# Combinations of the last two head pairs moved into the output projection, raw output weights through three fixed buffers

## The chip, the cores and the metric

The kernel runs on 1 core of one Trainium2 chip. The metric is device time in microseconds (us) of one execution of the whole program; of several runs the median is given. A profiled execution is one more run, with its own time. The engines are called as the profile calls them: PE is TensorE (PEld its weight loads), DVE is VectorE, ACT is ScalarE, POOL is GpSimd, SP is SyncE, which issues nearly all DMAs here, in order.

## The reference

One decoder layer for 2048 tokens of width 1024 in float32: a mixer of two groups of heads side by side, then a feed-forward part, then a last norm. Cut to what matters:

```python
def dilated_mixer(q, k, v, rel_bias):            # 8 heads of width 64
    outs, lses = [], []
    for window, dilation in ((128, 1), (512, 4), (2048, 16)):
        o, lse = dilated_branch(q, k, v, rel_bias, window, dilation)
        outs.append(o)
        lses.append(lse)
    w = softmax(stack(lses), axis=0)             # weights of the three branches
    return sum(w[..., None] * stack(outs), axis=0)

def reference(x, ...):
    gq, gk, gv, gr, glow, dq, dk, dv = split(rmsnorm(x) @ w_in)
    o_a = gated_linear_attention(gq, gk, gv, glow)   # "GLA": 4 heads, normed and gated
    o_b = dilated_mixer(dq, dk, dv, rel_bias)
    h = x + concat([o_a, o_b]) @ w_out               # the output projection
    h = h + square(relu(rmsnorm(h) @ w_ff1)) @ w_ff2
    return rmsnorm(h)
```

The step that is moved is the weighted sum at the end of `dilated_mixer`; the weights whose loading changes are `w_out`.

## The kernel before, in words

The kernel has four parts: the input projection, attention, the output projection (with the norm behind it), and the feed-forward part with the last norm. The first and the last issue their instructions in an order written out by hand (`manual_schedule`). In attention and in the output projection, where the change lies, the scheduling framework orders each engine's instructions when the program is built: the order of the code gives priorities, a model of times says what is ready, and `tc.keep_in_program_order` (lines 1042, 1048, 1055) pins an instruction to its place on its engine. On the chip each engine then runs its own list strictly in order.

**Precision.** Large matrix products are made of three: each operand is split into a high part (ACT, a copy to fp32r) and a low part (DVE, the rest), and `mm3` (lines 131 to 134) adds high x high, low x high and high x low in a PSUM bank. PSUM banks have tags; tag "o", used by GLA, has one bank.

**Memory.** Most SBUF tiles come from one pool of 26 equal slots (`slot`, line 119). An instruction whose tile has no free slot waits until an earlier tile's last reader is done.

**Attention** runs 160 units of four or two blocks of 128 queries. In round k, unit k + 3 gets its scores (lines 964, 966; DVE adds the bias and finds the extreme in L976, ACT takes the exponential in L977), unit k is transposed (L986, evicted in L993 or L995) and unit k - 2 is multiplied with the values (L1005, evicted in L1008 to a tile O per pair of heads and branch). Heads go in pairs `pr` 0 to 3, with branches `br` 2, 1, 0. `plan` holds other work by round (`at_unit`). Steps of GLA, one chain of small products, are mixed in at a fixed rate: L1131 starts a step's decay in the bank of tag "o", L1191 (DVE) reads the previous product from it.

**Combination.** When a pair of heads has its three branches, `combine` (line 1033) sums them with their weights, for n tiles of 128 tokens from tile t0. Branches 1 and 2 come back from DRAM (`combine_load`, L1030, tile `cmb`); branch 0 is still in O. The steps are: the minimum M of the three stored extremes (DVE, L1042, L1043), differences (L1045), Exp (ACT, L1048), the sum of weighted denominators Z (L1049 to L1052), its reciprocal (DVE, L1055), the weights (L1057), then for each four tiles three products (L1063) and two sums (L1065) of 128x512 elements, and for pairs 0 to 2, or the upper half of pair 3, a store to `mixD` in DRAM. All but M, Exp and the reciprocal run on POOL, except for tiles 12 to 15 of pair 3, which run on DVE (`W`, `X`). `combine` is a generator: each call of `step` (line 1257) runs it to the next `yield`. Pairs 0 to 2 are combined while the next pair is in attention (line 1283, eight tiles at a time), pair 3 in four pieces of four tiles at the end (line 1291).

**Output weights.** `load_wo` (line 1199) is called eight times, every third unit from unit 132 on. Each call takes a slot for the raw block, loads it (L1203) and splits it (ACT L1205 or L1208, DVE L1206 or L1209).

**Output projection.** Tiles go in the order 0, 4, 1, 5, 2, 6, 3, 7, then 8, 12, and so on; `mix_T` loads a tile one step ahead (L1393, L1394, tile `mx`), transposes it (L1385; for tokens below 1024 the last 128 columns come straight from pair 3's O) and splits it into `mT` (ACT L549, DVE L550). The product is lines 132 to 134 with the tiles `wo` and `mT`, the sum with x is L1554. After each tile `norm_to_T` normalizes the tile before it: square on ACT (L168), a power of -1/2 on POOL (L163), scaling on DVE (L170), transposes (L1385), copies `bb` (L1348). The feed-forward part follows; it isn't touched.

Of the kernel before, what the change touches and what calls it, by code (L numbers as in the profile page):

```python
# [18 lines left out]
D = 1024  # L19
# [87 lines left out]
def emit(tc, a, stop=99):  # L107
# [924 lines left out]

    def combine(pr, t0, n, loaded, X):

        ts = slice(t0, t0 + n)
        R = [outs[pr, 0][:, ts], *[r[:, t0 % 8:t0 % 8 + n] for r in loaded]]
        at = small[:, t0 // 4 % 2 * 48:] if n == 4 else small
        E, Z, M = view(at, (3, n, 2)), view(at[:, 6 * n:], (2, n, 2)), view(at[:, 10 * n:], (n, 2))
        nm = [r[:, :, 130:132] for r in R]
        den = [r[:, :, 0:130:129] for r in R]  # L1040
        W = V if (pr, t0) == (3, 12) else G
        tc.keep_in_program_order(V.tensor_tensor(M, nm[0], nm[1], op=OP.min))  # L1042
        V.tensor_tensor(M, M, nm[2], op=OP.min)  # L1043
        for b in range(3):
            W.tensor_tensor(E[:, b], M, nm[b], op=OP.subtract)  # L1045
        if pr < 3:
            yield
        tc.keep_in_program_order(A.activation(E, E, AF.Exp))  # L1048
        W.tensor_tensor(Z[:, 0], E[:, 0], den[0], op=OP.mult)  # L1049
        for b in (1, 2):  # L1050
            W.tensor_tensor(Z[:, 1], E[:, b], den[b], op=OP.mult)
            W.tensor_tensor(Z[:, 0], Z[:, 0], Z[:, 1], op=OP.add)  # L1052
        if pr < 3:
            yield
        tc.keep_in_program_order(V.reciprocal(Z[:, 1], Z[:, 0]))  # L1055
        for b in range(3):
            W.tensor_tensor(E[:, b], E[:, b], Z[:, 1], op=OP.mult)  # L1057
        yield
        for t in range(0, n, 4):
            rs = [r[:, t:t + 4, 1:129].rearrange("p t (h e) -> p t h e", h=2) for r in R]  # L1060
            for b, r in enumerate(rs):
                wb = E[:, b, t:t + 4].unsqueeze(3).to_broadcast([128, 4, 2, 64])
                X.tensor_tensor(r, r, wb, op=OP.mult)  # L1063
                if b:
                    X.tensor_tensor(rs[0], rs[0], r, op=OP.add)  # L1065
                    yield
        if pr < 3 or t0 >= 8:
            issue_later(3 if pr < 3 else 2,
                        mixD[:, 512 + 128 * pr:640 + 128 * pr].rearrange("(t p) n -> p t n", p=128)[:, ts],
                        R[0][:, :, 1:129])  # L1070
# [127 lines left out]

    def load_wo(n):
        for c in range(len(WO), len(WO) + n):  # L1200
            raw = slot("woraw")[:, :D]
            w = view(slot("wo", FR), (2, D))
            SP.dma_start(raw, wo[:, c])  # L1203
            if c < 4:
                A.activation(w[:, 0], raw, AF.Copy, scale=gn[:, c:c + 1])  # L1205
                V.scalar_tensor_tensor(w[:, 1], raw, gn[:, c:c + 1], w[:, 0].bitcast(F32), op0=OP.mult, op1=OP.subtract)  # L1206
            else:
                A.activation(w[:, 0], raw, AF.Copy)  # L1208
                V.tensor_tensor(w[:, 1], raw, w[:, 0].bitcast(F32), op=OP.subtract)  # L1209
            WO.append(w)  # L1210

# [37 lines left out]

    got, running = {}, {}  # L1250

    def combine_at(pr, t0, n, at, steps):

        if at is not None:
            at_unit(at + AHEAD, lambda: got.update({(pr, t0 // 8): combine_load(pr, t0 // 8)}))

        def step():
            if (pr, t0) not in running:
                running[pr, t0] = combine(pr, t0, n, got[pr, t0 // 8], V if (pr, t0) == (3, 12) else G)
            next(running[pr, t0], None)  # L1260

        for k in steps:
            at_unit(k + AHEAD, step)

    for pr in range(4):
# [3 lines left out]
        for hh, br in seq:  # L1269
# [7 lines left out]
            if br == 2 and first:  # L1277
                pieces = load_head(b.h)
                for n in (13, 11, 8):
                    at_unit(first - n, lambda p: next(p), pieces)  # L1280
                if hh == 0:
                    for half in range(2):
                        combine_at(pr - 1, 8 * half, 8, first - 2 + 7 * half, [first + 4 + 7 * half + n for n in range(8)])
            if (pr, br) != (3, 0):
                for n in range(0, NT, m):
                    units.append(Unit(b, range(n, n + m)))
            elif hh:
                for n in range(0, NT, 4):
                    for w in (was, b):
                        units.extend(Unit(w, range(n + k, n + k + 2)) for k in (0, 2))  # L1290
                for n, at in ((0, 8), (4, 11), (8, 14), (12, 18)):
                    combine_at(3, n, 4, first + 5 + n // 8 if n % 8 == 0 else None, [first + at + k for k in range(4)])
            was = b
    NU = len(units)
    for i in range(8):
        at_unit(NU - 28 + 3 * i + AHEAD, load_wo, 1)
    gla = gla_steps()
# [240 lines left out]
    nxt = mix_T(tiles[0])  # L1538
    late = None
    back = []  # L1540
    for at, t in enumerate(tiles):
# [13 lines left out]
        SP.dma_start(hD[t * 128:t * 128 + 128], h)  # L1555
        if late is not None:
            norm_to_T(*late)
        if back:
# [5 lines left out]
        if at == W1AT + 1:  # L1564
# [6 lines left out]
            sum1(0, 1)  # L1571
        late = (h, u[:, 0], t)

# [177 lines left out]
    with tc.manual_schedule(engines={SP.engine}):  # L1751
# [3 lines left out]
        for at in range(7):  # L1755
            if at == 2:
                norm_to_T(*late)
            if back:
# [120 lines left out]
```

## Time and profile before

| what | value |
|---|---|
| median of 3 runs | 2266.61 us (2266.53 to 2270.08) |
| profiled execution | 2268.76 us |
| its span, first to last instruction | 2267.0 us |
| busy time of ACT, DVE, POOL | 1163.6, 1628.3, 800.3 us |
| mean granted PE clock | 0.995 of full speed |
| attention's last value products (L1005) | end at about 858.5 us |
| output projection | from 858.4 to about 1070 us |

Rows of a timeline give the start in us from the span's start, the busy time in us, the engine, the line of the kernel, the operation, the tile written and the tiles read, shapes and count; in square brackets stands how long the engine was idle before it and what ended that. In the list of waits, a row gives who waited, for whom, the total in us, how often, and the longest. In a table of stretches, each engine's busy time stands with the number of its instructions, then the granted PE clock (1.00 is full speed), the mean busy share of the DMA engines, and GB/s. Groups give the count, the total busy time and the mean of one in ns, then idle time before them.

### The profile page before, as it was taken

What the parts mean: (1) busy time and instruction counts of PE and PEld (TensorE: products, weight loads), DVE (VectorE), ACT (ScalarE), POOL (GpSimd) and SP (SyncE); (2) the same over time, 40 slices, a digit from 0 to 9 for tenths busy, and PEclk for the clock granted to TensorE, in tenths of its full rate; (3) what the DMA queues carried; (4) which work ended last, traced back from release to release, by engine and by line L of the source; (5) the groups of instructions that cost most, each with busy time, mean ns of one, the idle gap of its engine ahead of it and who ended that gap; (6) DMA issues with size and microseconds to landing.
All of it is one profiled execution on the core that took longest, in us unless ns stands there. A gap on an engine that the chain in (4) does not pass through costs nothing.

```text
span 2267.0 us, 34335 instructions
## 1 busy us (share of the span) xinstructions
PE 2235.2 (99%) x12324; PEld 1928.8 (85%) x12324; DVE 1628.3 (72%) x2773; ACT 1163.6 (51%) x2088; POOL 800.3 (35%) x786
## 2 busy tenths in 40 slices
PE   9999999999999998999999999999999999999998
PEld 7978998899999997888888887888888788888886
DVE  6866767746677685446677779777776878758897
ACT  5554446425777772224655557555562333323544
POOL 2111000115478775000032335232345536332665
PEclk9999999999999999999999999999999999999999
DMA  7256444757757864777444456544488554454563
GB/s 206 87 176 194 131 136 153 251 175 236 229 186 252 270 196 144 222 229 260 131 151 140 149 195 206 154 138 150 137 271 313 192 166 135 148 160 156 169 222 112
DMA packets 308268, 415.24 MB, mean 183 GB/s; under 512 B 19509, under 2 KB 236126, under 8 KB 302464
## 3 DMA queue, kind: packets, MB, share of 16 engines
q1 hardware_dynamic: 307950, 412.77, 56.9%
q8 instruction: 97, 1.59, 0.3%
q14 instruction: 75, 0.61, 0.1%
q10 hardware_dynamic: 146, 0.27, 0.0%
HBM read 268.48 MB, written 149.20 MB: 184 GB/s over the span
## 4 chain that ended last, share of the span: by engine, by line
PE 88%; DVE 5%; DMA 2%; issue 2%; ACT 1%; POOL 1%; SPq 0%; POOLq 0%; ACTq 0%; DVEq 0%
PE ps_a L133 10%; PE ps_a L134 10%; PE ps_a L132 10%; PE ps_c L132 8%; PE ps_c L134 8%; PE ps_c L133 8%; PE ps_a L1005 5%; PE ps_d L134 4%; PE ps_d L132 4%; PE ps_d L133 4%; PE ps_d L986 3%; PE ps_c L966 2%; PE ps_c L964 2%; PE ps_o L132 2%; DVE ct L1650 2%
## 5 line engine op out<-in xcount | busy, mean ns | idle before, releaser
L1429 ACT ACTIVATE w1comb<-w1raw 128x512 fp32r<-128x512 f32 x224 | 141.4, 632 | 243.7 <-PE ps_a L134 81.8
L1608 ACT ACTIVATE cs<-rs 128x1024 fp32r<-128x1024 f32 x104 | 109.6, 1055 | 222.9 <-PE ps_c L134 127.9
L1434 DVE TENSOR_TENSOR w1comb<-w1raw,w1comb 128x512 fp32r<-128x512 f32 x224 | 175.8, 786 | 27.3 <-ACT w1comb L1429 27.3
L977 ACT ACTIVATE pe<-pe,O 128x256 f32<-128x256 f32 (+1 forms) x384 | 156.2, 454 | 58.0 <-DVE O L976 53.3
L1005 PE MATMUL ps_a<-v,pt 128*128 128x65 f32 x1200 | 180.3, 252 | 0.0
L1005 PEld LDWEIGHTS ps_a<-v,pt 128*128 128x128 f32 x1200 | 174.9, 194 | 1.1
L986 PE MATMUL ps_d<-ident,pe 128*128 128x128 f32 x600 | 159.9, 279 | 0.0
L976 DVE CUSTOM_DVE_ANT_0 pe<-ps_c,nb 128x256 f32<-128x256 f32 (+1 forms) x384 | 126.7, 361 | 41.9 <-PE ps_d L986 19.0
L163 POOL TENSOR_TENSOR stats<-stats,mhalf 128x1 f32<-128x1 f32 (+1 forms) x64 | 50.0, 783 | 299.9 <-DVE stats L162 299.9
L132 PE MATMUL ps_a<-hb,w1comb 128*128 128x512 f32 x384 | 149.6, 390 | 0.0
L133 PE MATMUL ps_a<-hb,w1comb 128*128 128x512 f32 x384 | 149.6, 390 | 0.0
L134 PE MATMUL ps_a<-hb,w1comb 128*128 128x512 f32 x384 | 149.4, 389 | 0.0
L1650 DVE TENSOR_TENSOR ct<-rt,ct 128x1024 fp32r<-128x1024 f32 x68 | 137.3, 2019 | 15.7 <-ACT ct L1646 15.4
L134 PE MATMUL ps_c<-ct,cs 128*128 128x512 f32 x360 | 140.1, 389 | 0.0
L132 PE MATMUL ps_c<-ct,cs 128*128 128x512 f32 x360 | 140.1, 389 | 0.0
L133 PE MATMUL ps_c<-ct,cs 128*128 128x512 f32 x360 | 140.1, 389 | 0.0
L918 POOL CAST qp<-qs 128x512 fp32r<-128x512 f32 x64 | 67.2, 1133 | 179.6 <-DVE acc L373 162.6
L1534 POOL TENSOR_TENSOR acc<-acc 128x256 f32<-128x256 f32 x75 | 69.0, 931 | 161.2 <-DVE acc L1534 148.6
L293 ACT ACTIVATE wcomb<-wraw 128x512 fp32r<-128x512 f32 (+2 forms) x119 | 89.2, 755 | 62.0 <-DVE wraw L305 27.0
L1615 DVE SCALAR_TENSOR_TENSOR cs<-rs,cs 128x1024 fp32r<-128x1024 f32 (+1 forms) x56 | 94.1, 1687 | 27.8 <-ACT cs L1608 27.6
L986 PEld LDWEIGHTS ps_d<-ident,pe 128*128 128x128 f32 x600 | 109.5, 187 | 0.3
L1534 POOL TENSOR_TENSOR xt<-acc,acc 128x256 f32<-128x256 f32 x32 | 28.2, 882 | 227.0 <-ACT acc L1496 210.2
(439 smaller groups left out, 7337.7 us busy)
## 6 DMA issues: line engine op xcount, KB each, us to landing
rs<-actD SPq DMA_DIRECT2D x103, 512.0 KB, 3.7
actD<-acc SPq DMA_DIRECT2D x288, 128.0 KB, 2.8
w1raw<-w_ff SPq DMA_DIRECT2D x32, 1024.0 KB, 6.6
rt<-w_ff SPq DMA_DIRECT2D x24, 1024.0 KB, 7.1
k<-kD SPq DMA_DIRECT2D x16, 1024.0 KB, 8.4
rb<-hTD SPq DMA_DIRECT2D x13, 1024.0 KB, 7.8
wraw<-w_in SPq DMA_DIRECT2D x12, 1024.0 KB, 5.4
cmb<-boD SPq DMA_DIRECT2D x16, 528.0 KB, 6.5
```

Source lines behind the costliest of these rows:

```text
L132: T.matmul(out, sh, mh, start=first, stop=False, skip_group_check=more)
L133: T.matmul(out, sl, mh, start=False, stop=False, skip_group_check=more)
L134: T.matmul(out, sh, ml, start=False, stop=last, skip_group_check=more)
L976: V.tensor_tensor_reduce(p, s, bias, scale=1.0, scalar=BIG, op0=OP.add, op1=OP.min, accum_out=nm)
L977: A.activation(p, p, AF.Exp, bias=nm, scale=-1.0)
L986: T.transpose(pb[:, i * 128:i * 128 + 128], src, ident)
L1005: T.matmul(self.b.opsum[:, n % 4], self.pt[:, i * 128:i * 128 + 128], self.b.v[:, blk, cols], start=first, stop=last)
L1429: A.activation(c[:, 0], v, AF.Copy)
L1434: V.tensor_tensor(c[:, 1], v, c[:, 0].bitcast(F32), op=OP.subtract)
L1534: (G if pool or all_pool[0] else V).tensor_tensor(t[l], t[x], t[y], op=OP.add if op == "+" else OP.subtract)
L1608: A.activation(v[:, 0], x, AF.Copy, scale=float(PRODUCTS[ph // 2][2]))
L1650: V.tensor_tensor(v[:, 1], x, v[:, 0].bitcast(F32), op=OP.subtract)
```

## The change

It does five things.

1. The combination of tiles 12 to 15 of pair 3 runs on POOL like all others.
2. The combinations of tokens 1024 to 2047 of pairs 2 and 3 are called from the loop of the output projection: pair 2 (eight tiles) after output tiles 1 to 3, three steps each; pair 3's tiles 8 to 11 after the fourth, and 12 to 15 after the fifth, all four steps at once. Their stores are issued there by a call of `issue` per output tile. The load of pair 2's upper half moves from unit 125 to 148.
3. In pairs 0 to 2 there is one more step, empty, between the sum Z and the reciprocal, and the second half of a pair starts eight units after the first, not seven.
4. The raw output weights no longer take a slot each. They go through three buffers in turn: the tile `xt` (idle in this part) and the halves of one slot.
5. The load of a raw block stands five units ahead of its split.

```diff
-    def combine(pr, t0, n, loaded, X):
+    def combine(pr, t0, n, loaded):
...
-        W = V if (pr, t0) == (3, 12) else G
...
-            W.tensor_tensor(E[:, b], M, nm[b], op=OP.subtract)
+            G.tensor_tensor(E[:, b], M, nm[b], op=OP.subtract)
...
         if pr < 3:
             yield
+        if pr < 3:
+            yield
         tc.keep_in_program_order(V.reciprocal(Z[:, 1], Z[:, 0]))
...
-                X.tensor_tensor(r, r, wb, op=OP.mult)
+                G.tensor_tensor(r, r, wb, op=OP.mult)
                 if b:
-                    X.tensor_tensor(rs[0], rs[0], r, op=OP.add)
+                    G.tensor_tensor(rs[0], rs[0], r, op=OP.add)
                     yield
...
-    def load_wo(n):
-        for c in range(len(WO), len(WO) + n):
-            raw = slot("woraw")[:, :D]
-            w = view(slot("wo", FR), (2, D))
-            SP.dma_start(raw, wo[:, c])
...
+    wo_raws = []
+
+    def load_wo(c):
+        if not wo_raws:
+            t = slot("woraw")
+            wo_raws.extend((xt, t[:, :D], t[:, D:2 * D]))
+        SP.dma_start(wo_raws[c % 3], wo[:, c])
+
+    def split_wo(c):
+        raw, w = wo_raws[c % 3], view(slot("wo", FR), (2, D))
...
         for k in steps:
-            at_unit(k + AHEAD, step)
+            if k < 0:
+                late.setdefault(-k, []).append(step)
+            else:
+                at_unit(k + AHEAD, step)
...
-                        combine_at(pr - 1, 8 * half, 8, first - 2 + 7 * half, [first + 4 + 7 * half + n for n in range(8)])
+                        at = [first + 4 + 8 * half + n for n in range(9)]
+                        combine_at(pr - 1, 8 * half, 8, first - 2 + (8 if pr < 3 else 30) * half,
+                                   at if pr < 3 or not half else [-1, -1, -1, -2, -2, -2, -3, -3, -3])
...
-                for n, at in ((0, 8), (4, 11), (8, 14), (12, 18)):
-                    combine_at(3, n, 4, first + 5 + n // 8 if n % 8 == 0 else None, [first + at + k for k in range(4)])
+                for n, at in ((0, 8), (4, 11), (8, -4), (12, -5)):
+                    combine_at(3, n, 4, first + 5 + n // 8 if n % 8 == 0 else None,
+                               [first + at + k if at > 0 else at for k in range(4)])
...
-        at_unit(NU - 28 + 3 * i + AHEAD, load_wo, 1)
+        at_unit(NU - 33 + 3 * i + AHEAD, load_wo, i)
+        at_unit(NU - 28 + 3 * i + AHEAD, split_wo, i)
...
         SP.dma_start(hD[t * 128:t * 128 + 128], h)
-        if late is not None:
-            norm_to_T(*late)
+        for f in late.get(at + 1, ()):
+            f()
+        issue(clock[0] + 99)
+        if last is not None:
+            norm_to_T(*last)
```

More of the change, by code (lines that the diff above doesn't have):

```diff
@@ L1048, in combine @@
         tc.keep_in_program_order(A.activation(E, E, AF.Exp))
-        W.tensor_tensor(Z[:, 0], E[:, 0], den[0], op=OP.mult)
+        G.tensor_tensor(Z[:, 0], E[:, 0], den[0], op=OP.mult)
         for b in (1, 2):
-            W.tensor_tensor(Z[:, 1], E[:, b], den[b], op=OP.mult)
-            W.tensor_tensor(Z[:, 0], Z[:, 0], Z[:, 1], op=OP.add)
+            G.tensor_tensor(Z[:, 1], E[:, b], den[b], op=OP.mult)
+            G.tensor_tensor(Z[:, 0], Z[:, 0], Z[:, 1], op=OP.add)
+        if pr < 3:
+            yield
         if pr < 3:
@@ L1056, in combine @@
         for b in range(3):
-            W.tensor_tensor(E[:, b], E[:, b], Z[:, 1], op=OP.mult)
+            G.tensor_tensor(E[:, b], E[:, b], Z[:, 1], op=OP.mult)
         yield
@@ L1197, in emit @@
     WO = []
-    def load_wo(n):
-        for c in range(len(WO), len(WO) + n):
-            raw = slot("woraw")[:, :D]
-            w = view(slot("wo", FR), (2, D))
[L1203 to L1210, printed above, removed]
+    wo_raws = []
[6 more added lines that the diff above has]
+        raw, w = wo_raws[c % 3], view(slot("wo", FR), (2, D))
+        if c < 4:
+            A.activation(w[:, 0], raw, AF.Copy, scale=gn[:, c:c + 1])
+            V.scalar_tensor_tensor(w[:, 1], raw, gn[:, c:c + 1], w[:, 0].bitcast(F32), op0=OP.mult, op1=OP.subtract)
+        else:
+            A.activation(w[:, 0], raw, AF.Copy)
+            V.tensor_tensor(w[:, 1], raw, w[:, 0].bitcast(F32), op=OP.subtract)
+        WO.append(w)
     pairs, outs = {}, {}
@@ L1248, in at_unit @@
         plan.setdefault(n, []).append(f)
-    got, running = {}, {}
+    got, running, late = {}, {}, {}
     def combine_at(pr, t0, n, at, steps):
@@ L1258, in step @@
             if (pr, t0) not in running:
-                running[pr, t0] = combine(pr, t0, n, got[pr, t0 // 8], V if (pr, t0) == (3, 12) else G)
+                running[pr, t0] = combine(pr, t0, n, got[pr, t0 // 8])
             next(running[pr, t0], None)
         for k in steps:
-            at_unit(k + AHEAD, step)
+            if k < 0:
+                late.setdefault(-k, []).append(step)
+            else:
+                at_unit(k + AHEAD, step)
     for pr in range(4):
@@ L1538, in emit @@
     nxt = mix_T(tiles[0])
-    late = None
+    last = None
     back = []
@@ L1571, in emit @@
             sum1(0, 1)
-        late = (h, u[:, 0], t)
+        last = (h, u[:, 0], t)
     w2 = a["w_ff2"].rearrange("o (c q p) n -> q p (o c) n", q=4, p=128)
@@ L1756, in emit @@
             if at == 2:
-                norm_to_T(*late)
+                norm_to_T(*last)
             if back:
```

## The prediction

> **What bounds the kernel now.** I read the page first, then who TensorE waited for, then stretches of the span, then the instructions around each of TensorE's two stops.
>
> ```profile
> span 2267.0 us, 34335 instructions
> ...
> PE 2235.2 (99%) x12324; PEld 1928.8 (85%) x12324; DVE 1628.3 (72%) x2773; ACT 1163.6 (51%) x2088; POOL 800.3 (35%) x786
> ```
>
> TensorE (PE) is busy 2235.2 of 2267.0 us. The change leaves its matmuls alone, so it can only win where PE stands still, or where its clock is low after it stood still. In the list of PE's waits, two of the first three lines lie where this change works (the second, L1479, belongs to the feed-forward part):
>
> ```profile
> PE ps_a L133 <- DVE mT L550: 5.6, 1, 5.6
> PE ps_d L132 <- ACT acc L1479: 3.4, 1, 3.4
> PE ps_o L1131 <- issue: 2.7, 1, 2.7
> ```
>
> The stretches (columns: length, busy PE, PEld, DVE, ACT, POOL, granted clock, DMA share, GB/s):
>
> ```profile
> 340.00:820.00 480.00, 480.00 (x3776) 454.91 (x3776) 329.42 (x1096) 298.21 (x739) 220.90 (x307) 1.00 0.67 216
> 831.65:834.30 2.65, 0.00 (x0) 0.03 (x1) 2.38 (x4) 1.53 (x5) 2.65 (x3) 1.00 1.10 351
> 834.30:838.60 4.30, 4.30 (x27) 4.30 (x28) 3.05 (x14) 4.15 (x11) 4.30 (x6) 0.60 1.17 316
> 872.78:877.00 4.22, 4.21 (x12) 3.38 (x13) 0.66 (x2) 0.00 (x0) 3.48 (x6) 0.61 0.44 119
> 905.00:1070.00 165.00, 165.00 (x831) 139.31 (x830) 84.66 (x123) 52.29 (x91) 7.14 (x13) 1.00 0.73 234
> ```
>
> From 340 to 820 (attention) and from 905 to 1070 (output projection) PE never stops and its clock is full: nothing can be won there, and anything new that holds PE up is a loss. The stop at 831.65 costs 2.65 us and then a slow clock, 4.30 us at 0.60: 4.30 x 0.40 = 1.72. After the second stop the clock is 0.61 for 4.21 busy us: 4.21 x 0.39 = 1.64.
>
> **The first stop** is made by the raw output weights; SP's queue, then ACT, DVE and PE:
>
> ```profile
> 825.20 0.57 SPq L1203 DMA_DIRECT2D woraw<-w_out  x1
> ```
>
> ```profile
> 830.78 1.06 ACT L1208 ACTIVATE wo<-woraw 128x1024 fp32r<-128x1024 f32 x1 [2.96 <-DMA woraw<-w_out]
> ```
>
> ```profile
> 831.87 1.56 DVE L1209 TENSOR_TENSOR wo<-woraw,wo 128x1024 fp32r<-128x1024 f32 x1 [2.18 <-ACT wo L1208]
> 833.36 0.84 DVE L1191 TENSOR_TENSOR gla<-gla,ps_o 64x256 f32<-64x256 f32 x2
> ```
>
> ```profile
> 834.30 0.68 PE L1131 MATMUL ps_o<-gla 128*128 128x130 f32 x4 [2.65 <-issue]
> ```
>
> The load goes out at 825.20 and lands 5.6 us later, at a DMA share above 1. ACT waits for it 2.96 us, DVE (in order behind ACT's result) another 2.18, L1191 stands behind DVE's split, and L1131 needs the one ps_o bank that L1191 reads. The trace says only "issue" for that last step; that it is the bank follows from the code and from L1191 ending at 834.20.
>
> **The second stop** is the handoff to the projection. PE, then ACT, DVE and POOL:
>
> ```profile
> 864.72 0.60 PE L1385 MATMUL ps_c<-ident,mx 128*128 128x128 f32 x4
> 865.41 0.33 PE L1385 MATMUL ps_d<-ident,O 128*128 128x128 f32 x1
> 866.49 0.73 PE L132 MATMUL ps_a<-wo,mT 128*128 128x512 f32 x2 [0.75 <-ACT mT L549]
> 872.78 0.80 PE L133 MATMUL ps_a<-wo,mT 128*128 128x512 f32 x1 [5.56 <-DVE mT L550]
> ```
>
> ```profile
> 865.85 0.59 ACT L549 ACTIVATE mT<-ps_d 128x512 fp32r<-128x512 f32 x1
> ```
>
> ```profile
> 870.61 0.68 DVE L550 TENSOR_TENSOR mT<-ps_c,mT 128x512 fp32r<-128x512 f32 x1
> 871.21 0.92 DVE L1065 TENSOR_TENSOR O<-O,cmb 128x512 f32<-128x512 f32 x1
> 872.05 0.68 DVE L550 TENSOR_TENSOR mT<-ps_d,mT 128x512 fp32r<-128x512 f32 x1
> ```
>
> ```profile
> 864.05 1.30 POOL L1065 TENSOR_TENSOR O<-O,cmb 128x512 f32<-128x512 f32 x1
> ```
>
> PE waits for the low part (L550) of tile 0's second half. Its high part was ready at 866.44, so DVE could have begun then; it began at 872.05, because DVE was working off the combination of tokens 1536 to 2047, of which the row at 871.21 is a part, and the low part of another tile (870.61). PE lost 0.75 + 5.56 = 6.31 us. Before that, the transpose of O (865.41) waited for POOL's last add of the combination of tokens 0 to 511, which ended at 864.05 + 1.30 = 865.35.
>
> All that is to be had is 2.65 + 1.72 + 6.31 + 1.64 = 12.3 us.
>
> **Part by part.**
>
> *Weights.* Each load moves five units ahead of its split. From the first of these issues to the one at 835.99 it is six loads, three units apart:
>
> ```profile
> 785.74 0.33 SPq L1203 DMA_DIRECT2D woraw<-w_out  x1
> ```
>
> ```profile
> 829.57 1.61 SPq L1030 DMA_DIRECT2D cmb<-boD  x2
> 831.23 2.60 SPq L1123 DMA_DIRECT2D gla<-gvD  x1
> 833.93 1.96 SPq L1030 DMA_DIRECT2D cmb<-boD  x2
> 835.99 8.95 SPq L1203 DMA_DIRECT2D woraw<-w_out  x2
> 845.43 0.33 SPq L1336 DMA_DIRECT2D gs<-mlp_norm_g  x1
> ```
>
> ```profile
> SPq L1203 <- PE ps_c L966: 10.3, 2, 6.4
> ```
>
> (835.99 - 785.74) / 18 = 2.8 us a unit, so five units are 14 us, against 2.96 us of lateness. The load of block c overwrites the buffer of block c - 3, whose split is planned four units earlier, 11 us. The loads no longer wait on SP for a slot (10.3 us in two waits, with later loads queued behind). So the first stop goes: 4.37 us. If the load is late all the same, nothing of that is won.
>
> *Combination of tokens 1536 to 2047 off DVE, and three combinations behind the first output tiles.* What remains at the handoff is the chain behind POOL: transpose of O 0.33 (from 865.41), ACT 0.59, DVE 0.68, with the small gaps between them at 867.2. PE would run out at 864.72 + 0.60 = 865.3. Left over: 1.9 us instead of 6.31. It is less if POOL ends the combination of tokens 0 to 511 sooner, since the 8-tile combination that fills POOL from 830 to 845 and the one of tokens 1024 to 1535 have gone; at best it is 0. The clock after such a stop costs between 0 and the 1.72 of the 2.65 us stop; I take half, 0.85. So the second stop shrinks from 7.95 to about 2.75 (bounds 0 and 3.6).
>
> The Trainium skill, "TensorE: Matmul & The Clock Gate", section "Why this matters for your kernels", asks for no idle gaps above about 3 us, and its section "What's actually happening" has the clock fall after an idle window of about 3.4 us. This trace disagrees: a stop of 2.65 us was followed by 4.30 us at 0.60. By the page the first stop would be worth 2.65 alone, the leftover stop would cost no clock, and the sum below would be 8.7.
>
> *What those combinations cost later.* On POOL between 780 and 885:
>
> ```profile
> L1065 POOL TENSOR_TENSOR O<-O,cmb 128x512 f32<-128x512 f32 x14 | 19.4, 1392 | 0.1
> L1063 POOL TENSOR_TENSOR cmb<-cmb,small 128x512 f32<-128x512 f32 x14 | 16.2, 1185 | 0.0
> L1063 POOL TENSOR_TENSOR O<-O,small 128x512 f32<-128x512 f32 x7 | 7.2, 1045 | 0.0
> ```
>
> Four tiles cost 1.05 + 2 x 1.19 + 2 x 1.39 = 6.2 us; the three combinations 12.4 + 6.2 + 6.2 = 24.8 us, into a stretch where POOL was busy 7.14 of 165. Who stands behind them is each tile's power of -1/2 (L163), on the way to its normalized transposes:
>
> ```profile
> 893.48 0.56 POOL L163 TENSOR_TENSOR stats<-stats,mhalf 128x1 f32<-128x1 f32 x1 [10.79 <-DVE stats L162]
> ```
>
> ```profile
> 894.07 1.28 DVE L170 SCALAR_TENSOR_TENSOR mx<-mx,stats,gs 128x1024 f32<-128x1024 f32 x1 [0.67 <-POOL stats L163]
> ```
>
> ```profile
> 903.61 0.60 PE L1385 MATMUL ps_c<-ident,mx 128*128 128x128 f32 x4
> ```
>
> The scaled tile is ready at 895.35, the transposes run at 903.61: 8.3 us of cover. Batches of 6.2 fit. The 12.4 us batch, begun at about 892 and taken in one piece ahead of the power, ends at 904.4; power and scale bring it to 906.2: 2.6 us late, once, and up to 1.7 us of clock. I take nothing, since PE may have the next tile's matmuls in hand; 4.3 stays in the range. SP gets three stores more among the projection's loads; the rows they read are first wanted by the ninth tile. The minima, reciprocals and Exps among the output tiles are tiny, and DVE has half of that stretch free.
>
> *The extra step and the shifted combinations of the first pairs* lie where PE never waited (340 to 820): nothing, and with that cover gone at most a stop like the first.
>
> Sum: 4.37 + (7.95 - 2.75) = 9.6 us. The profiled execution took 2268.76 us (its span and 1.76 outside), 2.15 above the median of the runs, 2266.61. It would go to 2259.2, the median to 2257.0.
>
> **The rivals.**
>
> *One stop stays.* The two loads of the 8-tile combination now stand on SP just ahead of those for tokens 0 to 1023, on DMA engines that are full there. If they push them back by one such pair (833.93 - 829.57 = 4.4 us) and POOL's chain with them, PE resumes 4.4 us later than above and the handoff costs 1.9 + 4.4 + 1.64 = 7.9, as before: a gain of 4.4, 2262.2. If the weights are late and the handoff is cured, the gain is 5.2, 2261.4. For it: the DMA share of 1.1 to 1.17. Against: POOL gets 12.4 us of room ahead of that chain. It decides once tokens 0 to 511 are combined later than the 865.35 of now.
>
> *Slots run out: slower.* The pool has 26. When the last scores are issued I count: six for two heads' q and k, v, bias, two rings, four of GLA, branch 0 of the last pair (15); branch 0 of the third pair, three loaded combinations, the raw-weight slot (20); six split weight blocks (26). Full, as now, where SP waits for the scores to end (6.4 us) and goes on at 845.43. The scores free seven, and two weight blocks, the gains and two tiles' mx and mT want seven; but now two of the old holders keep theirs until the third output tile. If another tile's load takes one first and tile 0's transposed halves get theirs only from GLA's four, they come when GLA's last store has landed:
>
> ```profile
> 858.35 0.48 PE L132 MATMUL ps_a<-wo,mT 128*128 128x512 f32 x1
> ```
>
> ```profile
> 873.84 1.54 SPq L1082 DMA_DIRECT2D mixD<-gla  x1
> ```
>
> With the 5.6 us that the load of 825.20 took to land as an estimate for this store, 873.84 + 1.54 + 5.6 + 0.59 + 0.68 = 882.3 in place of 858.35: 23.9 us late, 1.6 of clock, less the 12.3 of both stops: 13.2 slower, 2279.8. It decides from one slot too few at that place; v and the rings, freed as the last values end at about 858.5, speak against it.
>
> *No effect on the order.* The scheduler may run combinations planned among the output tiles earlier, as it runs others later than planned. But minimum, Exp and reciprocal are pinned on DVE and ACT, so POOL can't start before them. I give this no chance of its own.
>
> **How the numbers follow.** Forecast (both stops go or shrink, 2254 to 2261): 0.60. One stop stays (2261 to 2264): 0.22. Slots, slower by over 0.2%: 0.10. Other small stops that eat the gain (2264 to 2270): 0.08. About 0.2%, 4.5 us, is what a measurement of this kernel can tell from no change; 2262.1 is the border. Faster: 0.60, and half of 0.22, less a little for the 4.3 us of the power: 0.69. Slower 0.11, same 0.20. The range goes from 2266.6 - 12.3, less half a us of scatter, to where one stop stays and a small one comes: 2253.8 to 2265.0.
>
> **What would show it.** In the changed profile, right: PE's wait at L1131 gone and L1208's wait for woraw with it; no combination on DVE but minima and reciprocals; the wait for L550 at the handoff 2 us or less; L1063 and L1065 on POOL among the first five output tiles; PE full in the projection. Wrong: a PE stop of over 4 us at the first output matmuls, SP or ACT waiting there for a slot, or PE waiting for transposes of mx with L163 late.

## The result, and the profile after

The changed kernel takes 2256.15 us (median of six runs, 2254.47 to 2256.67) beside 2266.57 us for the kernel before (six runs, 2265.08 to 2270.08): 10.4 us less, ratio 0.9951, 95% interval 0.9941 to 0.9962. The forecast was 2257.0 in a range of 2253.8 to 2265.0. The profiled execution took 2256.31 us, with a span of 2254.5 us.

The head of the page, for the changed kernel:

```profile
span 2254.5 us, 34335 instructions
...
PE 2229.1 (99%) x12324; PEld 1925.5 (85%) x12324; DVE 1605.4 (71%) x2757; ACT 1164.0 (52%) x2088; POOL 812.5 (36%) x802
```

PE runs the same 12324 matmuls and is the bound as before. Sixteen instructions went from DVE to POOL; DVE lost 22.9 us of busy time and POOL gained 12.2.

The list of PE's waits, after (lines are those of the changed kernel: L1398 is the transpose of `mx` or `O` that was L1385, L1189 the GLA product that was L1188, L1492 belongs to the feed-forward part):

```profile
PE ps_d L132 <- ACT acc L1492: 3.4, 1, 3.4
...
PE ps_c L1398 <- DMA mx<-mixD: 2.0, 1, 2.0
```

Both waits at which the forecast aimed are gone: there is no wait for L550 at the handoff, and none at the GLA product L1132 (L1131 before) behind the weights. One is new, 2.0 us for the load of tile 0's `mx`. The table of stretches, after:

```profile
831.00:835.00 4.00, 4.00 (x42) 4.00 (x40) 1.74 (x8) 1.84 (x5) 1.80 (x4) 1.00 1.05 317
...
838.00:853.00 15.00, 12.80 (x116) 12.22 (x115) 11.88 (x38) 10.03 (x23) 11.66 (x29) 1.00 1.08 370
853.00:880.00 27.00, 27.00 (x148) 23.16 (x148) 8.28 (x15) 6.00 (x17) 13.84 (x20) 1.00 0.18 63
880.00:905.00 25.00, 25.00 (x124) 20.87 (x124) 9.63 (x16) 5.45 (x10) 13.68 (x15) 1.00 0.62 193
905.00:1060.00 155.00, 155.00 (x787) 131.14 (x786) 81.90 (x122) 51.46 (x91) 24.54 (x44) 1.00 0.73 236
```

Where PE stood at 831.65 it now runs through. From 853 to 1060, handoff and projection, it never stops, and the clock is full. All that is left is 15.00 - 12.80 = 2.20 us between 838 and 853: 0.2 at L1189 and 2.0 at the transposes of tile 0.

To compare kernels I use two sums. The *stretch* runs from a store at the beginning of attention (L383, at 449.41 in the kernel before) to the last store of `hD`; PE's work in it is the same in every kernel here. The *stops* are what PE loses after that store: I cut 630 us into pieces of 2 us, and for each take 2 less the busy time (idle), and the busy time times 1 less the clock (slow clock). In the profile of before the stops are 9.06 idle + 3.31 slow = 12.37 us, the 12.3 of the prediction; after they are 2.20 + 0 = 2.20. The stretch went from 621.21 to 610.95 us. So 10.2 us of stops answer for 10.3 us of stretch. The two profiled executions differ by 12.45 us; the other 2.2 lie outside: 0.2 ahead of attention, 2.0 in the feed-forward part, which the change does not touch.

### The profile page after: what moved, and what is told of

The parts are those of the page before. It is cut to its first block, busy times and chain, and to the rows that moved or that the text cites. A ratio compares the mean times of both kernels' runs of the same rounds, so it can differ in the third digit from the quotient of the medians.

```text
span 2254.5 us, 34335 instructions
## 1 busy us (share of the span) xinstructions
PE 2229.1 (99%) x12324; PEld 1925.5 (85%) x12324; DVE 1605.4 (71%) x2757; ACT 1164.0 (52%) x2088; POOL 812.5 (36%) x802
## 3 DMA queue, kind: packets, MB, share of 16 engines
q8 instruction: 97, 1.59, 0.3%
## 4 chain that ended last, share of the span: by engine, by line
PE 91%; DVE 4%; issue 2%; DMA 1%; ACT 1%; POOL 0%; SPq 0%; POOLq 0%; ACTq 0%; DVEq 0%
PE ps_a L132 11%; PE ps_a L133 11%; PE ps_a L134 11%; PE ps_c L132 9%; PE ps_c L134 8%; PE ps_c L133 8%; PE ps_a L1005 5%; PE ps_d L133 4%; PE ps_d L132 4%; PE ps_d L134 4%; PE ps_d L986 3%; PE ps_c L966 2%; PE ps_c L964 2%; PE ps_o L132 2%; PE ps_o L134 2%; PE ps_o L133 2%
## 5 line engine op out<-in xcount | busy, mean ns | idle before, releaser
L1666 DVE TENSOR_TENSOR ct<-rt,ct 128x1024 fp32r<-128x1024 f32 x68 | 129.8, 1909 | 18.8 <-ACT ct L1662 18.8
L163 POOL TENSOR_TENSOR stats<-stats,mhalf 128x1 f32<-128x1 f32 (+1 forms) x64 | 50.0, 783 | 242.6 <-DVE stats L162 242.5
L1631 DVE SCALAR_TENSOR_TENSOR cs<-rs,cs 128x1024 fp32r<-128x1024 f32 (+1 forms) x56 | 100.0, 1793 | 29.6 <-ACT cs L1624 29.3
```

The costliest lines, as they stand in the source:

```text
L1631: V.scalar_tensor_tensor(v[:, 1], x, -1.0, v[:, 0].bitcast(F32), op0=OP.mult, op1=OP.subtract)
L1666: V.tensor_tensor(v[:, 1], x, v[:, 0].bitcast(F32), op=OP.subtract)
```

## The experiments

My theory: PE's two stops are the whole cost; the weights' part removes the first, GpSimd's part the second, and the gains add up. The rivals: one of the stops stays or comes back in another place, GpSimd is the new bound, or the combinations in the projection cost something. Each kernel's ratio is to runs of the kernel before on the same chip; the groups of runs were made on different chips, so ratios are compared and not medians. Stretch and stops are those of one execution, the profiled one. The row "before" is the profile that the prediction read.

| kernel | ratio to before, 95% interval | idle | slow clock | stops | stretch |
|---|---|---|---|---|---|
| before | 1 | 9.06 | 3.31 | 12.37 | 621.21 |
| w_only | 0.9995 [0.9987, 1.0004] | 7.37 | 3.57 | 10.94 | 621.42 |
| g_only | 0.9969 [0.9961, 0.9978] | 6.38 | 1.57 | 7.95 | 617.06 |
| w_and_g | 0.9981 [0.9973, 0.9990] | 5.81 | 1.60 | 7.41 | 618.50 |
| c_only | 0.9960 [0.9948, 0.9972] | 3.78 | 2.58 | 6.36 | 613.74 |
| p3_moved | 0.9976 [0.9968, 0.9985] | 3.94 | 1.70 | 5.64 | 616.13 |
| p2_moved | 0.9968 [0.9955, 0.9980] | 3.31 | 1.59 | 4.90 | 613.78 |
| no_step | 0.9960 [0.9948, 0.9972] | 3.20 | 1.58 | 4.78 | 613.22 |
| late_load | 0.9967 [0.9955, 0.9979] | 3.19 | 1.47 | 4.66 | 613.53 |
| after_again | 0.9953 [0.9940, 0.9965] | 3.02 | 1.58 | 4.60 | 613.42 |
| loads_later | 0.9957 [0.9943, 0.9970] | 1.79 | 1.69 | 3.48 | 612.11 |
| gains_later | 0.9951 [0.9938, 0.9964] | 2.64 | 0.00 | 2.64 | 611.47 |
| one_batch | 0.9957 [0.9945, 0.9969] | 2.58 | 0.00 | 2.58 | 611.23 |
| the change | 0.9951 [0.9941, 0.9962] | 2.20 | 0.00 | 2.20 | 610.95 |

An interval is some 5 us wide, so the ratios part the first kernels from the last; to tell 2 us apart takes the stops and the stretch. These come from single executions: the changed kernel itself had 2.20 us of stops in one and 4.60 in another. The profiled executions of c_only and p3_moved were the slowest of theirs (3.8 and 4.3 us above the median), though some 3 us of that lie outside the stretch and in none of these sums; that of late_load was its fastest (2.1 below).

### The weights alone (w_only)

The kernel before, with parts 4 and 5 of the change (three fixed buffers, load five units ahead of split) and nothing else:

```diff
-            raw = slot("woraw")[:, :D]
+            t = slot("woraw")
+            wo_raws.extend((xt, t[:, :D], t[:, D:2 * D]))
...
-        at_unit(NU - 28 + 3 * i + AHEAD, load_wo, 1)
+        at_unit(NU - 33 + 3 * i + AHEAD, load_wo, i)
+        at_unit(NU - 28 + 3 * i + AHEAD, split_wo, i)
```

> The kernel before with the change to the weights alone: three fixed buffers, and each load five units ahead of its split; all combinations where they were. My theory (the first stop is the late landing of a raw block, the second is DVE's combination ahead of L550): the stop at L1131 is gone, the handoff still waits some 5.6 us for L550: 2266.6 - 4.4 = 2262.2 us. Rival (the first stop comes from GpSimd's and the DMA engines' load of the 8-tile combination at that time, and the wait for the weights only hides it): the stop stays in another form, 2265.5 to 2267.

Measured: no change, 0.9995, where I had expected 4.4 us. The first stop is gone, but nearly nothing is won. PE's waits in this kernel (L1391 is the transpose of tile 0's last columns from `O`):

```profile
PE ps_a L133 <- DVE mT L550: 2.7, 1, 2.7
PE ps_d L1391 <- POOL O L1065: 2.1, 1, 2.1
...
PE ps_a L132 <- ACT mT L549: 0.7, 1, 0.7
```

The transpose of `O` waits 2.1 us for POOL's last sum for tokens 0 to 511, the second of these two:

```profile
862.86 2.50 POOL L1065 TENSOR_TENSOR O<-O,cmb 128x512 f32<-128x512 f32 x2
```

L549 follows, and L550 is still held up by DVE's sums, 2.7 us. Counted from the start of the stretch, the sum ends 1.6 us later than in the kernel before (417.5 and 415.9), and PE, with the same matmuls behind it, runs out of work only 0.5 us earlier (415.4 and 415.9). So the first stop did not simply move to the second. By the pieces, its 4.3 us are gone, the handoff costs 9.1 us in place of 8.1, and small stops that the kernel before did not have add 1.8; the other 2.0 us are lost ahead of the handoff, where the same matmuls take longer though PE counts as busy. The stretch is as long as before.

### GpSimd alone (g_only)

The kernel before, with tiles 12 to 15 of pair 3 combined on POOL, in their old place:

```diff
-        W = V if (pr, t0) == (3, 12) else G
+        W = G
...
-                running[pr, t0] = combine(pr, t0, n, got[pr, t0 // 8], V if (pr, t0) == (3, 12) else G)
+                running[pr, t0] = combine(pr, t0, n, got[pr, t0 // 8], G)
```

> The kernel before with one edit: the combination of tiles 12 to 15 of the last pair on GpSimd, at its old place. My theory for the handoff (L550 stands behind DVE's combination): the 5.6 us wait for L550 goes, PE resumes when GpSimd's chain, ACT and DVE are through, the first stop stays: 2266.6 - 5.2 = 2261.4 us. Rival (GpSimd is the bound of the handoff, and gets 6.2 us more to do): no gain or a loss, 2266 to 2270.

Measured: 0.9969, which is 7.0 us, and 4.4 by the stops, 4.2 by the stretch. PE's waits, and then the low part of tile 0's second half on DVE:

```profile
PE ps_o L1131 <- issue: 2.8, 1, 2.8
...
PE ps_c L1385 <- DMA mx<-mixD: 1.8, 1, 1.8
...
PE ps_a L132 <- ACT mT L549: 1.1, 1, 1.1
```

```profile
866.25 0.68 DVE L550 TENSOR_TENSOR mT<-ps_d,mT 128x512 fp32r<-128x512 f32 x1
```

The first stop is as before (2.8), and of the second 1.1 is left: L549 ends at 866.09, and L550 follows it at once when DVE has no sums in front of it. That DVE's combination held L550 up is shown. New is a 1.8 us wait for the load of `mx`, the one that the changed kernel has too.

### Both, with no combination moved (w_and_g)

> Weights through fixed buffers and tiles 12 to 15 of pair 3 on GpSimd, every combination at its old place. Theory 1 (both stops are cured by these two parts; the combinations moved into the projection are there only to make room): as the changed kernel, 0.995, about 10 us less than before, no PE stop of more than 2.5 us at the handoff. Theory 2 (the move is needed: with the weights' stop gone, PE reaches the handoff some 2 us earlier and waits for GpSimd's last sums of tokens 0 to 511, as in the kernel with the weights' change alone): O's transpose waits 2 to 4 us for L1065, and the time is 2 to 5 us above the changed kernel's, 0.9965 to 0.9975.

This is the kernel before with the edits of w_only and of g_only together. Measured: 0.9981, which is 4.3 us, 5.0 by the stops and 2.7 by the stretch: at most half of what the whole change brings. The wait that theory 2 forecast is there; PE's wait, and the sum that it is for:

```profile
PE ps_d L1391 <- POOL O L1065: 2.6, 1, 2.6
```

```profile
867.85 1.27 POOL L1065 TENSOR_TENSOR O<-O,cmb 128x512 f32<-128x512 f32 x1
```

But its reason holds only in part. Counted from the start of the stretch, PE runs out of work at the handoff 0.5 us earlier than in the kernel before, not 2, and POOL's last sum for tokens 0 to 511 ends 2.0 us later (417.9 and 415.9). In the changed kernel it ends at 408.5. So the moved combinations are no mere tidying: without them POOL's sums are late at the handoff. Why they come later here than in the kernel before, no run shows.

### The combinations, with the old weights (c_only)

The changed kernel with `load_wo` as before (a slot for each raw block, loaded where it is split):

```diff
-            t = slot("woraw")
-            wo_raws.extend((xt, t[:, :D], t[:, D:2 * D]))
...
+            raw = slot("woraw")[:, :D]
...
-        at_unit(NU - 33 + 3 * i + AHEAD, load_wo, i)
-        at_unit(NU - 28 + 3 * i + AHEAD, split_wo, i)
+        at_unit(NU - 28 + 3 * i + AHEAD, load_wo, 1)
```

> The changed kernel with the old weights: a slot for each raw block, loaded and split in the same unit; the combinations behind the output tiles as in the change. My theory: ACT's wait for a raw block and the stop behind it stay or come back, the handoff is as in the changed kernel: 2256.2 + 4.4 = 2260.6 us. Rival (the combinations made both stops): about 2256.

Measured: 0.9960, between the changed kernel and the others. The interval takes in the changed kernel's ratio, so the times alone do not exclude the rival; the profile does. The stop on the weights has moved, and is larger. PE's wait and then SP and ACT:

```profile
PE ps_a L1005 <- ACT pt L993: 3.8, 1, 3.8
```

```profile
839.87 1.46 SPq L1204 DMA_DIRECT2D woraw<-w_out  x2
```

```profile
846.48 1.06 ACT L1209 ACTIVATE wo<-woraw 128x1024 fp32r<-128x1024 f32 x1 [3.96 <-DMA woraw<-w_out]
```

The last raw blocks are loaded at 839.87, ACT stands 4.0 us for them, and a copy behind that split (L993) holds PE up for 3.8 us, with 2.58 of slow clock. In return PE, coming later, no longer waits for `mx`. Net, that is 4.2 us of stops more than in the changed kernel's first profile and 1.8 more than in its second, and 2.8 and 0.3 us of stretch; the ratios are 2 us apart. So with the handoff mended, the weights' part is worth something from 0.3 to 4 us; alone it had shown at most 1.4.

### Which of the moved combinations counts (p2_moved, p3_moved)

p2_moved is the changed kernel with tiles 8 to 15 of pair 3 back in attention; p3_moved with pair 2's upper half back there instead.

```diff
-                for n, at in ((0, 8), (4, 11), (8, -4), (12, -5)):
+                for n, at in ((0, 8), (4, 11), (8, 14), (12, 18)):
```

```diff
-                        combine_at(pr - 1, 8 * half, 8, first - 2 + (8 if pr < 3 else 30) * half,
-                                   at if pr < 3 or not half else [-1, -1, -1, -2, -2, -2, -3, -3, -3])
+                        combine_at(pr - 1, 8 * half, 8, first - 2 + 8 * half, at)
```

> The changed kernel, but only pair 2's upper half is combined among the output tiles; tiles 8 to 15 of pair 3 stand in attention again. Stops and slow clock from the start of attention to the last output tile came to 12.4 us in the kernel before, 7.4 with weights and GpSimd alone and no combination moved, 2.2 to 4.6 in the changed kernel. Theory 1 (the eight tiles of pair 2, 12.4 us of GpSimd, held up the combination of tokens 0 to 511): about 2 to 5 us of stops, ratio 0.995 to 0.996. Theory 2 (the tiles of pair 3 mixed in between did it): 6 to 8 us of stops, O's transpose waits for GpSimd's last sum, ratio 0.9975 to 0.9985.

> The changed kernel, but only tiles 8 to 15 of pair 3 are combined among the output tiles; pair 2's upper half stands in attention again. Theory 1 (pair 2's eight tiles held up tokens 0 to 511): 6 to 8 us of stops, O's transpose waits for GpSimd's last sum by 2 to 4 us, ratio 0.9975 to 0.9985. Theory 2 (the tiles of pair 3 did it): 2 to 5 us of stops, 0.995 to 0.996.

Measured: p2_moved 0.9968 with 4.90 us of stops, all of them at the load of `mx` and the small stop ahead of it; p3_moved 0.9976 with 5.64. p2_moved's ratio lies above theory 1's range, p3_moved's inside it with its stops a little below. The intervals overlap, so the profile decides. In p3_moved, POOL (the second row is the sum for which PE waits):

```profile
863.42 2.05 POOL L1064 TENSOR_TENSOR cmb<-cmb,small 128x512 f32<-128x512 f32 x2
865.43 1.28 POOL L1066 TENSOR_TENSOR O<-O,cmb 128x512 f32<-128x512 f32 x1
866.66 1.01 POOL L163 TENSOR_TENSOR stats<-stats,mhalf 128x4 f32<-128x4 f32 x1
```

and PE in the same kernel:

```profile
PE ps_d L1397 <- POOL O L1066: 0.9, 1, 0.9
```

The sum ends at 866.7, from the start of the stretch as late as in the kernel before (416.5 and 415.9), and PE waits 0.9 us for it. In p2_moved there is no wait for POOL at all. So it is pair 2's upper half, 12.4 us of POOL ahead of pair 3's, that had to go. The wait for POOL was smaller than the 2 to 4 us I had written down.

### Is it the five units, or the buffers? (late_load)

The changed kernel, with each raw block's load called in the unit that splits it:

```diff
-        at_unit(NU - 33 + 3 * i + AHEAD, load_wo, i)
+        at_unit(NU - 28 + 3 * i + AHEAD, load_wo, i)
```

> The changed kernel with three fixed buffers, but each raw block loaded in the unit that splits it. My theory (the five units ahead are what hides the load): ACT waits for a raw block again and PE stops behind it, 2256.2 + up to 4.4 = 2260.6 us. Rival (what counts is that the loads no longer wait for a slot, or the scheduler sends them out early anyway as soon as their buffer is free): about 2256.

Measured: 0.9967 beside 0.9951 and 0.9953 for the changed kernel. The intervals overlap, but by the times alone my theory (2260.6 is a ratio of 0.9974) fits better than the rival (2256, 0.9953). The profiled execution speaks for the rival: its stops, 4.66, add up to what after_again has, 4.60 (0.77 of them are small ones between 783 and 787 that the changed kernel does not have), and ACT waits for no weights. SP and ACT in this kernel:

```profile
810.77 0.33 SPq L1206 DMA_DIRECT2D xt<-w_out  x1
815.77 0.33 SPq L1206 DMA_DIRECT2D woraw<-w_out  x1
```

```profile
838.87 1.05 ACT L1214 ACTIVATE wo<-xt 128x1024 fp32r<-128x1024 f32 x1
839.82 1.04 ACT L1214 ACTIVATE wo<-woraw 128x1024 fp32r<-128x1024 f32 x1
```

The loads go out 24 to 28 us ahead of their splits, though the code calls them in the same unit. With the five units it is the same (812.55 for a split at 840.75). A load into a fixed buffer waits for no slot, and the scheduler puts it on SP as soon as the buffer is read out: DVE's splits of the blocks that lay in these two buffers end at 810.74 and 815.74. SP's order is fixed when the program is built, so the loads stand as far ahead in every execution. The buffers hide the load, and these two loads do not need the five units. What made two of its six executions take 2264.4 us, 4.6 above the median, no trace shows; a cost of the missing units elsewhere is not excluded.

### What the 12.4 us batch costs (one_batch)

The changed kernel, with pair 2's upper half called behind the first output tile alone:

```diff
-                                   at if pr < 3 or not half else [-1, -1, -1, -2, -2, -2, -3, -3, -3])
+                                   at if pr < 3 or not half else [-1] * 9)
```

> The changed kernel, with all nine steps of pair 2's upper half behind the first output tile, instead of three behind each of three. My step (8.3 us of cover at the power L163, and PE with the next tile's products in hand): 0 us, L163 some 10 us late, no PE stop. Rival: PE waits for the scaled tile, 2.6 us of stop and up to 1.7 us of clock, so up to 4.3 us above the changed kernel.

Measured: 0.9957, the stops 2.58, none of them behind 850. Nothing is lost. POOL in this kernel:

```profile
875.13 4.05 POOL L1064 TENSOR_TENSOR cmb<-cmb,small 128x512 f32<-128x512 f32 x4
879.14 3.81 POOL L1066 TENSOR_TENSOR O<-O,cmb 128x512 f32<-128x512 f32 x3
882.90 0.57 POOL L163 TENSOR_TENSOR stats<-stats,mhalf 128x1 f32<-128x1 f32 x1
```

Counted from the start of the stretch, the batch began 6.3 us earlier than in the changed kernel, and the tile's power (L163) slipped in between its sums. In the changed kernel too the batch runs in one go but for one power (from 881.95 to 894.55), though its steps are called behind three tiles. So this experiment shows only that an earlier start costs nothing; a batch that keeps the power waiting to its end was not made.

### The extra empty step (no_step)

The changed kernel without the second `yield`, the second half again seven units after the first, and pair 2's upper half in eight steps behind the output tiles in place of nine.

> The changed kernel without the extra empty step of pairs 0 to 2, and the second half again seven units after the first. Mine: 0 us, since PE never waits in that part; the stops stay 2.2 to 4.6 us in sum. Rival: GpSimd's sums are late for DVE's reciprocal, which is pinned and stands in front of the scores' extremes and the copies: DVE idles and PE stops for it once or more, 1 to 4 us above the changed kernel.

Measured: 0.9960, stops 4.78. From 449 to 820 this kernel's PE is busy the whole time:

```profile
449.00:820.00 371.00, 371.00 (x3223) 362.74 (x3222) 250.43 (x976) 242.83 (x663) 218.39 (x304) 1.00 0.68 220
```

There was nothing for the step to mend, and its cost is below what the runs can tell.

### What makes the stop that is left (loads_later, gains_later)

In the changed kernel SP issues tile 0's `mx` behind the combination's load and two loads of gains, on DMA engines that are full (a busy share of 1.08 from 838 to 853). SP, then PE:

```profile
837.09 1.40 SPq L1030 DMA_DIRECT2D cmb<-boD  x2
839.11 2.14 SPq L1349 DMA_DIRECT2D gs<-mlp_norm_g  x1
841.30 0.43 SPq L1350 DMA_DIRECT2D gs<-final_norm_g  x1
...
843.09 0.88 SPq L1406 DMA_DIRECT2D mx<-mixD  x2
```

```profile
848.80 0.66 PE L1398 MATMUL ps_c<-ident,mx 128*128 128x128 f32 x4 [1.99 <-DMA mx<-mixD]
```

gains_later issues the two gains behind the first and the seventh output tile's loads; loads_later does so too, and puts the combination's load for tokens 1024 to 2047 of pair 3 behind the third output tile.

```diff
-    SP.dma_start(gM, bcast_row(a["mlp_norm_g"], D))
-    SP.dma_start(gF, bcast_row(a["final_norm_g"], D))
...
+        if at == 0:
+            SP.dma_start(gM, bcast_row(a["mlp_norm_g"], D))
+        if at == 6:
+            SP.dma_start(gF, bcast_row(a["final_norm_g"], D))
```

> The changed kernel, with the two loads of gains and the loads for tokens 1024 to 2047 of pair 3 issued behind the first output tiles. Theory 1 (the 2.0 us stop left at tile 0's transposes comes from these loads standing ahead of mx on SP and on full DMA engines): the stop goes, and the time is 2.0 to 2.2 us below the changed kernel's. Theory 2 (mx lands when it does because of its own slot or its own two reads): the stop stays, 0 us. A loss, if the copies of the gains or tokens 1024 to 1535 now come late in the projection: a PE stop behind gs or cmb, 2 us or more above the changed kernel.

> The changed kernel, with the two loads of gains behind the first output tiles and the combination's loads where they were. Theory 1 (mx of tile 0 lands late because the gains' 1 MB stand ahead of it on SP and the DMA engines): the 2.0 us stop shrinks to below 0.5, with no new stop at the output weights (that one came in the run that moved the combination's loads as well): 2.0 us below the changed kernel, at most 4.6 where its stop costs clock too. Theory 2 (the combination's loads ahead of mx are enough to make it late): the stop stays at 1.5 or more, and the time is the changed kernel's within 1 us.

Measured: loads_later 0.9957. The wait for `mx` is gone; but another stop took its place, ahead of it: ACT stands 4.85 us in front of an output weight's split, and PE 1.75 us behind that, with 1.69 of slow clock.

```profile
834.69 1.06 ACT L1214 ACTIVATE wo<-xt 128x1024 fp32r<-128x1024 f32 x1 [4.85 <-DMA cmb<-boD]
```

The raw block's load had gone out at 810.25, so it was not that. The split also needs a free slot for its result; what would have freed it I did not find. Nor does the vanished wait show by itself that the loads had made it: PE came to tile 0's transposes at 845.71, some 3.5 us late behind the new stop, and `mx` had landed shortly before, at about 845.0 (4.9 us after its second issue).

gains_later: 0.9951, the same as the changed kernel. `mx` goes out at 838.08, 3.6 us earlier from the start of the stretch, yet PE still waits for it, 1.78 and 0.77 us at the first two tiles:

```profile
844.73 0.63 PE L1396 MATMUL ps_c<-ident,mx 128*128 128x128 f32 x4 [1.78 <-DMA mx<-mixD]
```

That agrees with theory 2 in its numbers, but not in its reason. Counted from the start of the stretch, `mx` is there 2.7 us earlier than in the changed kernel (397.0 and 399.6), more than the stop; in loads_later about 1.5 us earlier. So the loads ahead of it do delay it, the gains among them. But in both kernels the framework also puts tile 0's transposes 16 matmuls earlier on PE (3433 stand ahead of them in the stretch, in the changed kernel 3449), and in gains_later PE comes there 2.5 us earlier. The wait stays because its other side moved too. What it would be with PE's order kept, neither run shows. No version beat the changed kernel by what a measurement can tell.

### The changed kernel once more (after_again)

> The changed kernel once more, beside the others of this call. Every theory: 10.4 us less than the kernel before (ratio 0.995), leftover stop of about 2.0 us at tile 0's transposes (L1398 behind the load of mx), clock full afterwards. If the leftover stop is gone or more than 4 us in this execution, it is scatter and not structure.

Measured: 0.9953, 2257.38 us. The stop at `mx` was 2.54 us in this execution, and this time the clock fell behind it:

```profile
846.00:848.00 2.00, 1.01 (x7) 1.01 (x8) 0.63 (x3) 0.26 (x1) 2.00 (x5) 0.86 1.03 397
848.00:850.00 2.00, 2.00 (x14) 2.00 (x13) 1.02 (x2) 1.31 (x4) 2.00 (x6) 0.50 1.05 417
850.00:852.00 2.00, 2.00 (x17) 2.00 (x17) 0.69 (x2) 0.38 (x1) 2.00 (x2) 0.78 0.85 339
```

0.14, 1.00 and 0.44 us (the 2.00, 2.00 and 1.01 us of busy time, each by its missing clock), 1.58 in sum, where the first profile had none.

## Why the prediction was right, and where it was not

**Right: the total, and that it lies in two stops.** 12.3 us were to be had, the stops of the profile before add to 12.37, and 10.2 of them went. I forecast 9.6; the medians say 10.4.

**Right, but not by itself: the first stop goes, 4.37.** It went, in w_only and in every kernel with the fixed buffers. But the sum counted it twice over: it takes 4.37 us for PE coming earlier, and then lets PE run out of work at the handoff at 865.3, as if it came no earlier, against a sum on POOL that ends at 865.35. By its own rows the leftover wait would have been some 4.4 us longer unless POOL ended earlier, and I had taken POOL's earlier end for a mere bonus. w_and_g, where POOL gets no room, gained 5.0 us of stops and not 9.6. In the changed kernel POOL's sum ends 7.4 us earlier (408.5 in place of 415.9 from the start of the stretch), which pays for the gap. That the forecast total held all the same is partly luck. By itself the weights' part is worth at most 1.4 us of stops (12.37 to 10.94), nothing in the stretch and nothing that the runs can tell; from the side of the changed kernel 1.8 to 4.2 us of stops (c_only). My rival of one remaining stop had it right that a chain on POOL would then decide, but priced it at 4.4 us of gain and up; w_only gives 1.1 by the ratio.

**Wrong as to the cause: the five units.** I let 14 us of planned lead hide the load. The plan's units do not set the time of the loads that late_load shows: they are issued 24 to 28 us ahead with the five units and without.

**Right in size, wrong in place: 1.9 us are left over.** I had the chain behind POOL's sum for tokens 0 to 511 leave 1.9 us at the handoff, with 0 as the best case, if POOL ended sooner. The best case came, and that 2.0 us are left all the same is luck. POOL and PE, after:

```profile
856.37 1.29 POOL L1066 TENSOR_TENSOR O<-O,cmb 128x512 f32<-128x512 f32 x1
```

```profile
860.47 0.27 PE L1398 MATMUL ps_d<-ident,O 128*128 128x128 f32 x1
```

The sum ends at 857.66, and the transpose runs at 860.47 without a wait: 2.8 us to spare. What is left, 2.0 us, is a load that the forecast did not have: the rival put SP's crowded queue in front of the loads for tokens 0 to 1023, and it was tile 0's `mx` that came late.

**The clock behind the leftover stop: taken at half, 0.85.** It was 0 in one profile of the changed kernel and 1.58 in the other. It is nearly all or nothing: behind a stop of 1.7 to 3.3 us it was either 0 or 1.5 to 1.7 (w_only, with three stops within 7 us, lost 3.57, and c_only, with one of 3.78, 2.58). Stops of 1.75 (loads_later) and 1.91 us (late_load) cost it, stops of 1.99 (the change) and 2.14 us (one_batch) did not, so length alone doesn't decide. The Trainium skill, "TensorE: Matmul & The Clock Gate", section "What's actually happening", has the clock follow a free-running window of about 3.4 us, and ties the moment of the change to where in that window the first matmul lands. If the place of a stop in the window counts in the same way, losses would be all or nothing; 3.4 us at half speed gives an estimate of 1.7 us from that page's figure, near the 1.5 to 1.7 here. But the same section has the clock fall after an idle window of about 3.4 us, and these stops are shorter than one; here the trace decides against it.

**Right: the late combinations cost nothing.** In the changed kernel, POOL and DVE:

```profile
883.96 4.05 POOL L1064 TENSOR_TENSOR cmb<-cmb,small 128x512 f32<-128x512 f32 x4
887.97 0.56 POOL L163 TENSOR_TENSOR stats<-stats,mhalf 128x1 f32<-128x1 f32 x1
888.50 6.05 POOL L1066 TENSOR_TENSOR O<-O,cmb 128x512 f32<-128x512 f32 x4
```

```profile
882.59 0.15 DVE L162 TENSOR_SCALAR stats<-stats 128x1 f32<-128x1 f32 x1 [1.25 <-ACT mx L168]
```

The power of the second tile could have run at 882.74 and ran 5.2 us later, behind products of the batch. That is less than the 8.3 us of cover, and PE is full in that stretch. The feared case, the power behind the whole batch of 12.4, did not come, not even in one_batch; what it would cost is not shown.

**Right: the extra step, 0** (no_step). **Slots did not run out** in the changed kernel: no stop from 853 to 1060.

What stays open: g_only gained 7.0 us by its ratio and 4.4 by its stops, and w_and_g, with one edit more, gained less by the runs (0.9981 against 0.9969, the intervals just meeting) and by the stretch (2.7 and 4.2 us). In w_only, w_and_g and p3_moved, the three with fixed buffers and pair 2's upper half in attention, the stretch is about 2 us longer than the stops account for (621.42 - 10.94 = 610.5, 618.50 - 7.41 = 611.1 and 616.13 - 5.64 = 610.5, against 608.8 before and 608.7 after); in c_only it is 1.4 us shorter. In w_only and w_and_g these 2 us are lost ahead of the handoff. What loses them, I did not find.

## What to carry to other kernels

Two stops that follow each other on the same engine are not two terms of a sum: when the first goes, the engine asks for the second stop's input sooner, and may gain nothing unless that input gets earlier too. Here half of the gain came only with the part that moved work from in front of POOL's sums. So ask of each stop what ends last once the one ahead of it is gone, and mend the chain of the last one first. An edit also moves what the framework places around it, as the transposes of tile 0 show, so look at both sides of a wait that stays. In these runs a load into a buffer of its own went out as soon as that buffer was read out, while one that takes a slot from a shared pool was held to the pool: to hide a load, give it the buffer before giving it lead.

## What the runs showed of the hardware

Two things I had not expected. PE's clock falls to half for about 3 us, or not at all, behind stops of nearly the same length: 1.91 us cost 1.47, and 1.99 cost nothing. A stop of 3.78 us (c_only) cost 2.58. And in the changed kernel, SP issued two `mx` loads at 843.09 whose data PE used only at 848.80, 5.7 us later, while the DMA engines moved 370 GB/s at a busy share of 1.08; with the gains out of the way it was 6.6 us (838.08 to 844.73), of which issuing the two took 2.8.
